# Band attention of the sample rows in plain float32, its four head pairs on four 32-column groups of the array

## The chip, the core and the metric

The kernel runs on one core of a Trainium2 chip. [...] The metric is the device time of one execution in microseconds (us). Three runs of the kernel before gave 1215.79, 1216.45 and 1216.54; the median is 1216.45.

## What is computed

One step of a streaming encoder layer: 512 prompt rows and 8 sample sequences of 16 new rows each, all float32. After one shared input projection there are two attention branches (A: latent attention; B: attention over a band of keys), then a gated merge, an output projection and a SwiGLU feed-forward part. The change lies in branch B of the sample rows. Each of the 8 sequences has 512 cached keys and values and 16 new ones, 8 heads of 64:

```python
def softmax_attend(q, k, v, bias):
    scale = q.shape[-1] ** -0.5
    s = jnp.einsum('bqhd,bkhd->bhqk', q, k).astype(jnp.float32) * scale + bias
    p = jax.nn.softmax(s, axis=-1).astype(v.dtype)
    return jnp.einsum('bhqk,bkhd->bqhd', p, v)

def band_sample(q, k_new, v_new, k_buf, v_buf, rel_bias, past_len):
    ...
    k = jnp.concatenate([k_buf, k_new], axis=1)
    v = jnp.concatenate([v_buf, v_new], axis=1)
    kpos = jnp.concatenate([past_len - W + jnp.arange(W), past_len + jnp.arange(Sd)])
    qpos = past_len + jnp.arange(Sd)
    return softmax_attend(q, k, v, band_bias(rel_bias, qpos, kpos)[None])
```

## The kernel before

Most products are not plain float32. An operand is split into a high part, rounded to the type float32r, and a low part, the rest (`split`, lines 83 to 89: a copy on ScalarE for the high part, a subtraction on VectorE for the low one), and a product is three matmuls: high by high, high by low, low by high (`mm3`, lines 91 to 94). Transposes go through TensorE (line 138) into PSUM tiles `tr` (4 of them); products go into PSUM tiles `mm` (4 of them). `granule` (line 178) loads 512 KB into one of three buffers `w_raw` and splits it.

The sample stage (from line 799) goes through the 8 sequences in one loop (line 1018). Each turn does the scores of one sequence for both branches and the values of the sequence before; the order of the operations is written out in a string (line 1019), and a scheduler may move instructions within what the dependencies allow. In the string, capital letters are work on this sequence, small ones on the one before:

- `N` (`band_start`, line 928): GpSimd copies the 16 queries of the sequence into the zeroed tiles `Qbd`, high and low. Per head pair the stationary is 128 x 128, of which 32 columns (2 heads x 16 queries) hold values; it takes two PSUM tiles for the scores.
- `K0` to `K3` (`band_keys`, line 937): per head pair, four transposes of cached keys, the split into `kTh` and `kTl`, and the 16 new keys by GpSimd (lines 947, 948).
- `S0` to `S3` (`band_scores`, line 951): per pair and half of the 528 keys three matmuls of 264 columns; the four pairs add up in one PSUM tile of 128 rows.
- `X` (`band_softmax`): bias, maximum, exponential, scaling by the sum (lines 961 to 964, 842 to 850, 646 to 650).
- `P` (`band_probs`, line 966): five transposes of the probabilities, split into pieces of 32 high and 32 low columns.
- `v0` to `v3` (`band_values`, line 977): per pair, five key blocks, the 64-column stationary against the high and the low part of the cached values (lines 987, 988); `o` (`band_out`, line 993): four transposes and the addition of the two parts.
- `K` without a digit, `Y`, `p`, `u`: keys, scores, transposed probabilities and values of the latent branch. `mla_values` (line 919) is in plain float32: its probabilities and cached latents are not split (line 924). In the first turn `absorb` (line 825) has plain float32 products too (line 834), on 64 rows of the array at a time: rows 0 to 63 for one set of four matmuls, rows 64 to 127 for the next.

The queries and new keys reach the stage transposed, with the other work of the projections, as `qbT`, `qbTl`, `kbT`, `kbTl` (`pair_T`, line 491).

```python
for op in "N K0 S0 v0 K1 v1 S1 K2 S2 v2 K3 S3 X p v3 K u o Y P A".split():
```

Of the kernel before, what the change touches and what calls it, by code (L numbers as in the profile page):

```python
# [9 lines left out]
F32R = mybir.dt.float32r  # L10
# [37 lines left out]
def layer_kernel(  # L48
# [47 lines left out]
    def rsqrt(out, ss, inv, pl, n):  # L96
        v = pl.tile([P, n], F32, tag="rs_v", bufs=2, name=nm("rsv"))
        t = pl.tile([P, n], F32, tag="rs_t", bufs=2, name=nm("rst"))
        if not isinstance(inv, list):
            inv = [(0, n, inv)]  # L100
        for a, b, sc in inv:
            V.tensor_scalar(out=v[:, a:b], in0=ss[:, a:b], scalar1=sc, scalar2=EPS, op0=ALU.mult, op1=ALU.add)
        # a square root of the scalar engine's table, then a Newton step to float32
        for a, b, sc in inv:
            S.activation(out=t[:, a:b], in_=ss[:, a:b], func=AF.Sqrt, scale=sc, bias=eps_t)
        V.reciprocal(out, t)
        V.tensor_tensor(out=t, in0=out, in1=out, op=ALU.mult)  # L107
        V.scalar_tensor_tensor(out=t, in0=t, scalar=-0.5, in1=v, op0=ALU.mult, op1=ALU.mult)
        V.scalar_tensor_tensor(out=out, in0=t, scalar=1.5, in1=out, op0=ALU.add, op1=ALU.mult)
# [10 lines left out]
    # ---------------------------------------------------------------- constants  # L120
# [10 lines left out]
    # the tensor engine's clock rises while the first loads are under way  # L131
# [29 lines left out]
    # weight staging: 0.5 MB granules, each split exactly into a high and a low part  # L161
# [58 lines left out]
    # ---------------------------------------------------------------- state of the sample up to its attention  # L220
# [6 lines left out]
    qbT, qbTl = sbt([P, 4, P], "qbT", F32R), sbt([P, 4, P], "qbTl", F32R)  # L227
    kbT, kbTl = sbt([P, 4, P], "kbT", F32R), sbt([P, 4, P], "kbTl", F32R)
# [25 lines left out]
    # ---------------------------------------------------------------- modulation, normed input, norms of cached keys  # L254
    with pool("klat") as kp, pool("xin") as xp:
# [79 lines left out]
        # h^T = xn^T * A + B, split  # L335
# [27 lines left out]
    # small constants of the attention part  # L363
# [38 lines left out]
    def split3(dst, src, order):  # L402
        # parts of src, 32 columns each, side by side: high and low parts in the order given
        first = order.index("h")
        hi = dst[:, :, first * 32:(first + 1) * 32]
        S.copy(hi, src)
        for i, o in enumerate(order):
            d = dst[:, :, i * 32:(i + 1) * 32]
            if o == "h" and i != first:
                S.copy(d, src)  # L410
            elif o == "l":
                V.tensor_tensor(out=d, in0=src, in1=f(hi), op=ALU.subtract)

    # ---------------------------------------------------------------- projections out of the modulated input
# [8 lines left out]
    with pool("cwork") as cw:  # L423
# [67 lines left out]
        def pair_T(hi, lo, src, scale):  # L491
            pt = tr_tile()
            for j in range(4):
                transpose(pt[:, j * P:(j + 1) * P], src[:, j * P:(j + 1) * P])
            split(hi, lo, pt.rearrange("p (j n) -> p j n", j=4), scale)

        def epi_qb(t, ps):
            qn = head_norm(ps)
            if t < 4:
                nc.sync.dma_start(qb_d[t * P:(t + 1) * P, :], qn)  # L500
            else:
                pair_T(qbT, qbTl, qn, gqb128)

        def epi_kb(t, ps):
# [7 lines left out]
            else:  # L512
                nc.sync.dma_start(bk_s[0].rearrange("s q h d -> (s q) (h d)"), kb)
                pair_T(kbT, kbTl, kb, None)
# [116 lines left out]
    # relative-bias table, its clipped far end extended, distance rising along the row  # L631
# [20 lines left out]
    # ---------------------------------------------------------------- attention of the prompt, beside the gates  # L652
# [5 lines left out]
    def gate_block(blk, pl):  # L658
        # sigmoid(z) = (1 + tanh(z / 2)) / 2; the sum and the factor come with the merge
# [25 lines left out]
    with pool("pwork") as pw:  # L685
# [17 lines left out]
        def head_in(n):  # L703
            br, h = n // H, n % H
            st = {"br": br, "h": h, "bias": None}
            if h % 2 == 0:
                vn = load_nat(vb_d if br else va_d, P, h // 2 * P, "vnat")
                # stationary of a head: its high and low parts side by side, the high part at the head's rows
# [90 lines left out]
    # ---------------------------------------------------------------- attention of the sample  # L799
    e2 = {}  # L800
    with pool("ework") as ew:
# [17 lines left out]
        Qbd = [et([P, 640], f"qbd{p}", 1, F32R) for p in range(2)]  # L819
        for q_ in Qbd:  # L820
            G.memset(f(q_), 0.0)
        vbh, vbl = et([P, 512], "vbh", 1, F32R), et([P, 512], "vbl", 1, F32R)
        split(vbh, vbl, vb_n)

        def absorb():
            # q' = Wk (g qn) per head
# [101 lines left out]
        def band_start(s):  # L928
            new = slice(s * DSEQ, (s + 1) * DSEQ)
            for p, src in ((0, qbT), (1, qbTl)):  # L930
                for h2 in range(2):
                    r = slice(64 * h2, 64 * h2 + 64)
                    G.tensor_copy(Qbd[p][r, :].rearrange("p (j x) -> p j x", x=160)[:, :, h2 * DSEQ:(h2 + 1) * DSEQ],
                                  f(src[r, :, new]))
            return {"s": s, "ps": [mm_tile(), mm_tile()]}

        def band_keys(st, pr_):
# [7 lines left out]
            hi, lo = et([P, KEYS], "kTh", 3, F32R), et([P, KEYS], "kTl", 3, F32R)  # L945
            split(hi[:, :PAST], lo[:, :PAST], pt)
            G.tensor_copy(hi[:, PAST:], f(kbT[:, pr_, new]))
            G.tensor_copy(lo[:, PAST:], f(kbTl[:, pr_, new]))
            st["k", pr_] = hi, lo

        def band_scores(st, pr_):
            hi, lo = st["k", pr_]
            ps_ = slice(pr_ * P, (pr_ + 1) * P)
            for hf in range(2):
                ks = slice(hf * KH, (hf + 1) * KH)
                mm3(st["ps"][hf][:, :KH], Qbd[0][:, ps_], Qbd[1][:, ps_], hi[:, ks], lo[:, ks], pr_ == 0, pr_ == 3)
# [9 lines left out]
        def band_probs(st):  # L966
            # per pair of heads: stationary [high | low] parts of its 32 rows of probabilities
            PT = et([P, 20, 2, 32], "PTb", 1, F32R)

            def evac(js, src):  # L970
                r, v = slice(4 * js.start, 4 * js.stop), src.rearrange("p j (a x) -> p (j a) x", x=32)
                split(PT[:, r, 0, :], PT[:, r, 1, :], v)

            probs_T(*st["P"], evac)
            st["PT"] = PT

        def band_values(st, pr_):
            if pr_ == 0:
                st["po"] = mm_tile()
            c = slice(pr_ * P, (pr_ + 1) * P)  # L980
            if pr_ % 2 == 0:
                st["v"] = granule(wa, cache_band_v[0, st["s"]].rearrange("(j p) h d -> p j (h d)", p=P)
                                  [:, :, pr_ * P:(pr_ + 2) * P], [4, 2 * P])
            vh, vl = [a[:, :, (pr_ % 2) * P:(pr_ % 2 + 1) * P] for a in st["v"]]
            for j in range(5):
                lhs = st["PT"][:, 4 * j + pr_].rearrange("p a x -> p (a x)")
                T.matmul(st["po"][:64, c], lhs, vh[:, j, :] if j < 4 else vbh[:, c], start=(j == 0), stop=False)
                T.matmul(st["po"][:64, c], lhs, vl[:, j, :] if j < 4 else vbl[:, c], start=False, stop=(j == 4))
            if pr_ == 3:
                st["o2"] = et([64, 512], "o2", 1)  # L990
                S.copy(st["o2"], st["po"][:64, :])

        def band_out(st):
            s = st["s"]
            pt = tr_tile()
            for pr_ in range(4):
                transpose(pt[:, pr_ * 64:(pr_ + 1) * 64], st["o2"][:, pr_ * P:(pr_ + 1) * P])
            pv = pt[:, :256].rearrange("p (j a x) -> p j a x", a=2, x=32)
            ol = et([P, 4, 32], "ol", 1)
            S.copy(ol, pv[:, :, 1, :])  # L1000
            c = slice(SEQ + s * DSEQ, SEQ + (s + 1) * DSEQ)
            for h2 in range(2):
                r, q = slice(64 * h2, 64 * h2 + 64), slice(h2 * DSEQ, (h2 + 1) * DSEQ)
                V.tensor_tensor(out=oT[1][r, :, c], in0=pv[r, :, 0, q], in1=ol[r, :, q], op=ALU.add)
# [8 lines left out]
        # operations of a step: lower case on the sequence before, upper case on this one  # L1013
# [4 lines left out]
        for s in range(NSEQ + 1):  # L1018
            for op in "N K0 S0 v0 K1 v1 S1 K2 S2 v2 K3 S3 X p v3 K u o Y P A".split():
                k, a = op[0], [int(c) for c in op[1:]]  # L1020
                if k.islower():
# [3 lines left out]
                    elif k == "v":  # L1025
                        take(1)
                elif s < NSEQ:
# [4 lines left out]
                    elif k == "S":  # L1032
                        band_scores(nxt, *a)
# [29 lines left out]
    # ---------------------------------------------------------------- merge of the branches  # L1063
# [18 lines left out]
    def gate_rows(c0, scale):  # L1082
        # rows of a gate, by tokens: of the prompt, of the sample
# [59 lines left out]
    # ---------------------------------------------------------------- output projection, residual, second norm  # L1143
# [79 lines left out]
    # ---------------------------------------------------------------- feed-forward  # L1223
# [61 lines left out]
def _tables():  # L1285
    """Rotary tables of the positions, and selectors of the modulation rows: of the shapes alone."""
# [40 lines left out]
```

## Time and profile before

| | |
|---|---|
| median of three runs | 1216.45 us |
| profiled execution, its span | 1215.7 us |
| TensorE busy | 1189.0 us, 98% |
| VectorE, ScalarE, GpSimd busy | 684.2, 544.3, 137.9 us |
| moved by DMA | 155.30 MB, 128 GB/s on average |
| turns of the sample stage after the first | 116.1 us, 15.25 us for one in the middle |

The profile is one execution. [...] The idle time shown in brackets is that just before an instruction, with what ended it.

### The profile page before, as it was taken

The numbers are of one execution on the slowest core, as the hardware profiler recorded it, in microseconds if no ns is written. First come the engines' busy times: TensorE is split into PE (matmuls) and PEld (weight loads), VectorE is DVE, ScalarE is ACT, GpSimd is POOL, SyncE is SP. The second block draws the span as 40 slices with busy tenths as digits, with TensorE's granted clock in tenths as the row PEclk, the third lists the DMA queues.
The fourth block names the chain that finished last, engine by engine and source line by source line (L and its number), as shares of the span: only waits on it lengthen the run. The fifth ranks groups of instructions, "written<-read, shape, count | busy, mean of one in ns | idle before, by whom it ended". The sixth has DMA issues, their size and how long they took to land. (4 is left out here: it accounts for less than half of the span.)

```text
span 1215.7 us, 19702 instructions
## 1 busy us (share of the span) xinstructions
PE 1189.0 (98%) x7515; PEld 1077.5 (89%) x7515; DVE 684.2 (56%) x1539; ACT 544.3 (45%) x1086; POOL 137.9 (11%) x253
## 2 busy tenths in 40 slices
PE   8889999999999999999999998999999999999998
PEld 6568988999987889899989888999989999889996
DVE  4887566858887775777766437433344233342333
ACT  6775533446776665666653246322112222112210
POOL 2440001010000101334212221000000000000000
PEclk9998999999999999999999998999999999999999
DMA  8651434475655348455367312322123222232111
GB/s 260 227 161 46 127 137 136 159 235 167 184 162 176 119 137 287 138 178 173 95 213 266 103 55 70 88 70 78 62 70 105 70 71 87 67 89 70 70 40 65
DMA packets 159264, 155.30 MB, mean 128 GB/s; under 512 B 24632, under 2 KB 123475, under 8 KB 159170
## 3 DMA queue, kind: packets, MB, share of 16 engines
q1 hardware_dynamic: 159170, 154.05, 40.4%
q8 instruction: 59, 0.97, 0.3%
q14 instruction: 35, 0.29, 0.1%
HBM read 135.15 MB, written 18.88 MB: 127 GB/s over the span
## 5 line engine op out<-in xcount | busy, mean ns | idle before, releaser
L85 ACT CAST whi<-wraw 128x1024 fp32r<-128x1024 f32 (+2 forms) x184 | 190.3, 1038 | 273.4 <-PE mm L94 107.5
L86 DVE TENSOR_TENSOR wlo<-wraw,whi 128x1024 fp32r<-128x1024 f32 (+3 forms) x168 | 203.4, 1213 | 131.6 <-ACT whi L85 127.3
L92 PE MATMUL mm<-h2T,whi 128*128 128x320 f32 x704 | 217.9, 311 | 0.0
L93 PE MATMUL mm<-h2Tl,whi 128*128 128x320 f32 x704 | 217.8, 310 | 0.0
L94 PE MATMUL mm<-h2T,wlo 128*128 128x320 f32 x704 | 217.8, 310 | 0.0
L92 PEld LDWEIGHTS mm<-h2T,whi 128*128 128x128 f32 x704 | 132.9, 189 | 0.4 <-ACT aT L85 0.4
L93 PEld LDWEIGHTS mm<-h2Tl,whi 128*128 128x128 f32 x704 | 132.7, 189 | 0.1
L94 PEld LDWEIGHTS mm<-h2T,wlo 128*128 128x128 f32 x704 | 132.7, 189 | 0.0
L1237 DVE TENSOR_TENSOR sg<-mm,sg 128x320 f32<-128x320 f32 x44 | 21.6, 492 | 121.3 <-PE mm L94 119.3
L93 PE MATMUL mm<-wlo,aT 128*128 128x512 f32 x220 | 85.5, 389 | 0.0
L92 PE MATMUL mm<-whi,aT 128*128 128x512 f32 x220 | 85.5, 389 | 0.0
L94 PE MATMUL mm<-whi,aTl 128*128 128x512 f32 x220 | 85.4, 389 | 0.0
L92 PE MATMUL mm<-hT_hi,whi 128*128 128x320 f32 x256 | 81.5, 318 | 0.0
L94 PE MATMUL mm<-whi,hT_lo 128*128 128x512 f32 (+3 forms) x240 | 79.6, 332 | 0.0
L94 PE MATMUL mm<-hT_hi,wlo 128*128 128x320 f32 x256 | 79.5, 311 | 0.0
L93 PE MATMUL mm<-hT_lo,whi 128*128 128x320 f32 x256 | 79.4, 310 | 0.0
L92 PE MATMUL mm<-whi,hT_hi 128*128 128x512 f32 (+3 forms) x240 | 79.4, 331 | 0.0
L93 PE MATMUL mm<-wlo,hT_hi 128*128 128x512 f32 (+3 forms) x240 | 79.4, 331 | 0.0
L1268 DVE TENSOR_TENSOR tmp<-mm,gate 128x512 f32<-128x512 f32 x30 | 20.7, 690 | 78.7 <-PE mm L94 78.7
L85 ACT CAST aT<-sg 128x320 fp32r<-128x320 f32 x44 | 20.0, 455 | 78.7 <-DVE sg L1237 78.7
L92 PEld LDWEIGHTS mm<-hT_hi,whi 128*128 128x128 f32 x256 | 48.2, 188 | 2.1 <-issue 1.2
L94 PEld LDWEIGHTS mm<-hT_hi,wlo 128*128 128x128 f32 x256 | 48.1, 188 | 1.2 <-DVE wlo L86 0.3
(343 smaller groups left out, 2672.4 us busy)
## 6 DMA issues: line engine op xcount, KB each, us to landing
wraw<-in_w_ada_dram SPq DMA_DIRECT2D x48, 512.0 KB
wraw<-in_w_in_dram SPq DMA_DIRECT2D x28, 512.0 KB
wraw<-in_w_gate_dram SPq DMA_DIRECT2D x22, 512.0 KB
wraw<-in_w_up_dram SPq DMA_DIRECT2D x22, 512.0 KB
wraw<-in_w_down_dram SPq DMA_DIRECT2D x22, 512.0 KB
lat<-in_cache_kv_latent_dram SPq DMA_DIRECT2D x16, 512.0 KB
wraw<-in_cache_band_v_dram SPq DMA_DIRECT2D x16, 512.0 KB
kn<-in_cache_band_k_dram SPq DMA_DIRECT2D x16, 512.0 KB
```

The source lines that it names most:

```text
L85: S.copy(hi, src)
L86: (eng or V).tensor_tensor(out=lo, in0=src, in1=f(hi), op=ALU.subtract)
L92: T.matmul(out, lh, rh, start=start, stop=False)
L93: T.matmul(out, lh, rl, start=False, stop=False)
L94: T.matmul(out, ll, rh, start=False, stop=stop)
L1237: V.tensor_tensor(out=sg, in0=pu[:, :HALF], in1=sg, op=ALU.mult)
L1268: V.tensor_tensor(out=tmp, in0=ps, in1=gate2[t // 4][:, cc], op=ALU.mult)
```

## The change

The band branch of the sample rows no longer splits anything. Queries and new keys are kept in plain float32 (`qbd`, `kbT`); `qbd` holds for each sequence and head pair a stationary of 128 rows and 32 columns, two blocks of 64 rows x 16 queries. The scores of a pair go to 32 rows of the PSUM tile of their own, which is a 32-column group of the array: pair 0 to rows 0 to 31, pair 3 to rows 96 to 127, one plain float32 matmul per pair and half, none adding to another. All eight come after the four pairs' keys. The transposed keys are one copy, by VectorE for even pairs and by ScalarE for odd ones, in six buffers. The probabilities are one copy; the values are loaded by halves of the keys instead of by halves of the heads, used as loaded, and each pair's product of 32 x 128 goes to its own 32 rows of one PSUM tile. The output is one transpose and two copies. The order of a step has two operations `v` instead of four and one `S` after the keys.

```diff
-    qbT, qbTl = sbt([P, 4, P], "qbT", F32R), sbt([P, 4, P], "qbTl", F32R)
-    kbT, kbTl = sbt([P, 4, P], "kbT", F32R), sbt([P, 4, P], "kbTl", F32R)
+    qbd, kbT = sbt([P, 4, NSEQ, 32], "qbd"), sbt([P, 4, P], "kbT")
+    G.memset(qbd, 0.0)
...
-                pair_T(qbT, qbTl, qn, gqb128)
+                pv = pair_T(qn).rearrange("p j (s q) -> p j s q", q=DSEQ)
+                for h2 in range(2):
+                    r = slice(64 * h2, 64 * h2 + 64)
+                    S.activation(out=qbd[r, :, :, h2 * DSEQ:(h2 + 1) * DSEQ], in_=pv[r], func=AF.Copy, scale=gqb128[r])
...
-                pair_T(kbT, kbTl, kb, None)
+                S.copy(kbT, pair_T(kb))
...
-        Qbd = [et([P, 640], f"qbd{p}", 1, F32R) for p in range(2)]
-        for q_ in Qbd:
-            G.memset(f(q_), 0.0)
-        vbh, vbl = et([P, 512], "vbh", 1, F32R), et([P, 512], "vbl", 1, F32R)
-        split(vbh, vbl, vb_n)
...
         def band_start(s):
-            new = slice(s * DSEQ, (s + 1) * DSEQ)
-            for p, src in ((0, qbT), (1, qbTl)):
-                for h2 in range(2):
-                    r = slice(64 * h2, 64 * h2 + 64)
-                    G.tensor_copy(Qbd[p][r, :].rearrange("p (j x) -> p j x", x=160)[:, :, h2 * DSEQ:(h2 + 1) * DSEQ],
-                                  f(src[r, :, new]))
-            return {"s": s, "ps": [mm_tile(), mm_tile()]}
+            return {"s": s}
...
-            hi, lo = et([P, KEYS], "kTh", 3, F32R), et([P, KEYS], "kTl", 3, F32R)
-            split(hi[:, :PAST], lo[:, :PAST], pt)
-            G.tensor_copy(hi[:, PAST:], f(kbT[:, pr_, new]))
-            G.tensor_copy(lo[:, PAST:], f(kbTl[:, pr_, new]))
-            st["k", pr_] = hi, lo
-
-        def band_scores(st, pr_):
-            hi, lo = st["k", pr_]
-            ps_ = slice(pr_ * P, (pr_ + 1) * P)
+            kT = et([P, KEYS], "kT", 6)
+            (S.copy if pr_ % 2 else V.tensor_copy)(kT[:, :PAST], pt)
+            G.tensor_copy(kT[:, PAST:], kbT[:, pr_, new])
+            st["k", pr_] = kT
+
+        def band_scores(st):
+            st["ps"] = [mm_tile(), mm_tile()]
             for hf in range(2):
-                ks = slice(hf * KH, (hf + 1) * KH)
-                mm3(st["ps"][hf][:, :KH], Qbd[0][:, ps_], Qbd[1][:, ps_], hi[:, ks], lo[:, ks], pr_ == 0, pr_ == 3)
+                for pr_ in range(4):
+                    T.matmul(st["ps"][hf][32 * pr_:32 * pr_ + 32, :KH], qbd[:, pr_, st["s"], :],
+                             st["k", pr_][:, hf * KH:(hf + 1) * KH], start=True, stop=True)
...
         def band_probs(st):
-            PT = et([P, 20, 2, 32], "PTb", 1, F32R)
-            def evac(js, src):
-                r, v = slice(4 * js.start, 4 * js.stop), src.rearrange("p j (a x) -> p (j a) x", x=32)
-                split(PT[:, r, 0, :], PT[:, r, 1, :], v)
-            probs_T(*st["P"], evac)
+            PT = et([P, 5, P], "PTb", 2)
+            probs_T(*st["P"], lambda js, src: S.copy(PT[:, js, :], src))
             st["PT"] = PT
...
-        def band_values(st, pr_):
-            if pr_ == 0:
+        def band_values(st, half):
+            if half == 0:
                 st["po"] = mm_tile()
-            c = slice(pr_ * P, (pr_ + 1) * P)
-            if pr_ % 2 == 0:
-                st["v"] = granule(wa, cache_band_v[0, st["s"]].rearrange("(j p) h d -> p j (h d)", p=P)
-                                  [:, :, pr_ * P:(pr_ + 2) * P], [4, 2 * P])
-            vh, vl = [a[:, :, (pr_ % 2) * P:(pr_ % 2 + 1) * P] for a in st["v"]]
-            for j in range(5):
-                lhs = st["PT"][:, 4 * j + pr_].rearrange("p a x -> p (a x)")
-                T.matmul(st["po"][:64, c], lhs, vh[:, j, :] if j < 4 else vbh[:, c], start=(j == 0), stop=False)
-                T.matmul(st["po"][:64, c], lhs, vl[:, j, :] if j < 4 else vbl[:, c], start=False, stop=(j == 4))
-            if pr_ == 3:
-                st["o2"] = et([64, 512], "o2", 1)
-                S.copy(st["o2"], st["po"][:64, :])
+            vt = load_raw(cache_band_v[0, st["s"], half * 2 * P:(half + 1) * 2 * P].rearrange("(j p) h d -> p j (h d)", p=P),
+                          [2, 512])[1]
+            for j in range(2 + half):
+                jj = 2 * half + j
+                for pr_ in range(4):
+                    c = slice(pr_ * P, (pr_ + 1) * P)
+                    T.matmul(st["po"][32 * pr_:32 * pr_ + 32, :P], st["PT"][:, jj, 32 * pr_:32 * pr_ + 32],
+                             vt[:, j, c] if j < 2 else vb_n[:, c], start=(jj == 0), stop=(jj == 4))
+            if half:
+                st["o2"] = et([P, P], "o2", 2)
+                S.copy(st["o2"], st["po"][:, :P])
...
-            for op in "N K0 S0 v0 K1 v1 S1 K2 S2 v2 K3 S3 X p v3 K u o Y P A".split():
+            for op in "N K0 K1 v0 K2 K3 v1 S X p K u o Y P A".split():
...
                     elif k == "v":
-                        take(1)
+                        take(2)
```

In `band_out` one transpose of 128 x 128 and two copies by ScalarE stand in place of four transposes, a copy and two additions. `take` fills the first turn with blocks of the gates' projection; four times one became two times two.

## Rows read from the trace of the kernel before

**Rows 1.** The page: busy us (share) and instructions; GB/s in 40 slices:

```profile
PE 1189.0 (98%) x7515; PEld 1077.5 (89%) x7515; DVE 684.2 (56%) x1539; ACT 544.3 (45%) x1086; POOL 137.9 (11%) x253
...
GB/s 260 227 161 46 127 137 136 159 235 167 184 162 176 119 137 287 138 178 173 95 213 266 103 55 70 88 70 78 62 70 105 70 71 87 67 89 70 70 40 65
```

**Rows 2.** Stretches: length, busy PE, PEld, DVE, ACT, POOL, clock, DMA share, GB/s:

```profile
545.05:560.30 15.25, 14.90 (x145) 14.46 (x145) 11.38 (x32) 10.47 (x24) 6.11 (x22) 1.00 0.53 174
...
500.30:616.40 116.10, 112.29 (x1077) 106.59 (x1077) 83.95 (x216) 77.53 (x165) 38.35 (x141) 1.00 0.48 149
```

**Rows 3.** Groups of TensorE in one step: busy us, mean ns, idle before:

```profile
L924 PE MATMUL mm<-PT,lat 128*128 128x128 f32 x16 | 2.3, 275 | 0.0
...
L924 PE MATMUL mm<-PT,lat_n 128*128 128x128 f32 x4 | 0.8, 275 | 0.0
```

**Rows 4.** TensorE in order of time: start us, length us, count, idle before:

```profile
547.24 0.22 PE L988 MATMUL mm<-wlo,PTb 128*64 128x128 f32 x1
547.30 0.23 PE L987 MATMUL mm<-whi,PTb 128*64 128x128 f32 x1
547.36 0.34 PE L93 MATMUL mm<-kTl,qbd 128*128 128x264 f32 x1
...
554.96 1.06 PE L924 MATMUL mm<-PT,lat 128*128 128x128 f32 x8
...
556.29 0.46 PE L138 MATMUL tr<-ident,o 64*128 64x64 f32 x4
556.68 0.39 PE L908 MATMUL mm<-krT,qrT 96*128 96x264 f32 x1
...
557.03 0.28 PE L93 MATMUL mm<-lTl,qp 128*128 128x264 f32 x1
...
558.12 0.28 PE L94 MATMUL mm<-lTh,qpl 128*128 128x264 f32 x1
...
558.91 1.04 PE L138 MATMUL tr<-ident,kn 128*128 128x128 f32 x8
560.30 0.51 PE L92 MATMUL mm<-kTh,qbd 128*128 128x264 f32 x2 [0.35 <-ACT kTh L85]
```

**Rows 5.** The same view around the plain float32 products of the first turn:

```profile
488.38 2.26 PE L834 MATMUL mm<-qnT,wkT 64*128 64x128 f32 x24
490.57 1.09 PE L138 MATMUL tr<-ident,lat 128*128 128x128 f32 x8
491.59 1.16 PE L834 MATMUL mm<-qnT,wkT 64*128 64x128 f32 x8
492.68 0.66 PE L138 MATMUL tr<-ident,rnb 128*128 128x128 f32 x4
```

**Rows 6.** Groups of VectorE, ScalarE and GpSimd in the same step:

```profile
L86 DVE TENSOR_TENSOR kTl<-tr,kTh 128x512 fp32r<-128x512 f32 x4 | 2.6, 682 | 1.2 <-ACT kTh L85 1.2
L86 DVE TENSOR_TENSOR wlo<-wraw,whi 128x1024 fp32r<-128x1024 f32 x2 | 2.4, 1222 | 0.0
...
L650 DVE TENSOR_SCALAR Pr<-Pr,sm 128x528 f32<-128x528 f32 x2 | 1.0, 498 | 0.6 <-DVE sm L649 0.5
...
L910 DVE CUSTOM_DVE_ANT_0 S<-mm,S 128x264 f32<-128x264 f32 x2 | 0.8, 426 | 0.0
...
L85 ACT CAST kTh<-tr 128x512 fp32r<-128x512 f32 x5 | 2.9, 602 | 2.1 <-POOL kTl L948 1.8 <-PE tr L138 0.4
L85 ACT CAST whi<-wraw 128x1024 fp32r<-128x1024 f32 x2 | 2.1, 1058 | 0.0
...
L947 POOL CAST kTh<-kbT 128x16 fp32r<-128x16 f32 x4 | 1.7, 463 | 0.0
```

**Rows 7.** VectorE and ScalarE in order of time, in the band's softmax:

```profile
555.86 0.14 DVE L844 TENSOR_REDUCE nmax<-mx 128x1 f32<-128x2 f32 x1
...
556.10 0.74 ACT L648 ACTIVATE Pr<-S,nmax 128x528 f32<-128x528 f32 x1 [0.64 <-DVE nmax L844]
```

More of the change, by code (lines that the diff above doesn't have):

```diff
@@ L489, in head_norm, with pair_T @@
             return qn
-        def pair_T(hi, lo, src, scale):
+        def pair_T(src):
             pt = tr_tile()
@@ L494, in pair_T @@
                 transpose(pt[:, j * P:(j + 1) * P], src[:, j * P:(j + 1) * P])
-            split(hi, lo, pt.rearrange("p (j n) -> p j n", j=4), scale)
+            return pt.rearrange("p (j n) -> p j n", j=4)
         def epi_qb(t, ps):
@@ L995, in band_out @@
             pt = tr_tile()
[L996 to L1000, printed above, removed]
+            transpose(pt[:, :P], st["o2"])
+            pv = pt[:, :P].rearrange("p (j x) -> p j x", x=32)
             c = slice(SEQ + s * DSEQ, SEQ + (s + 1) * DSEQ)
             for h2 in range(2):
-                r, q = slice(64 * h2, 64 * h2 + 64), slice(h2 * DSEQ, (h2 + 1) * DSEQ)
-                V.tensor_tensor(out=oT[1][r, :, c], in0=pv[r, :, 0, q], in1=ol[r, :, q], op=ALU.add)
+                r = slice(64 * h2, 64 * h2 + 64)
+                S.copy(oT[1][r, :, c], pv[r, :, h2 * DSEQ:(h2 + 1) * DSEQ])
         def step_0():
@@ L1032, in layer_kernel @@
                     elif k == "S":
-                        band_scores(nxt, *a)
+                        band_scores(nxt)
                     elif k == "X":
```

## The prediction

> **What bounds the kernel now.** I began with the busy times of the page: TensorE is busy 98% of the span [rows 1], so an instruction taken off it shortens the run unless something takes its place, and work taken off the other engines is worth little by itself. Then the stage that the change touches, stretch by stretch: eight sequences, a step of 15.25 us for each in the middle and 116.1 us for all but the first turn [rows 2]. [...] Next the groups of one step, for counts [rows 3], and the order of time, for what an instruction really takes from TensorE: not its duration (matmuls overlap) but the distance from one start to the next [rows 4].
>
> **What is removed, per sequence.** The old scores are 2 halves x 4 pairs x 3 products = 24 matmuls of 264 columns. Ten of the same shape stand in a row from 557.03 to 558.12, 0.121 us apart [rows 4]: 24 x 0.121 = 2.90 us. The old values are 4 pairs x 5 key blocks x 2 parts = 40 matmuls of 128 columns, 0.06 us apart [rows 4]: 2.40 us. The four transposes of the output take from 556.29 to 556.68, 0.39 us [rows 4]. Sum 5.69 us.
>
> **What is added, per sequence.** A plain float32 product in this stage is that of the latent values, L924. The code has 10 such matmuls per step, the trace 16 + 4 = 20 records [rows 3]: a float32 matmul is two records. Eight take 1.06 us, the last alone 0.28, so 0.112 us per record of 128 columns [rows 3, 4]. In proportion a record of 264 columns takes 0.23 us. The new scores are 8 matmuls = 16 records, the new values 20 matmuls = 40 records.
> What these cost hangs on how far the four column groups run at once. No row shows column groups. One end is none at once: 16 x 0.23 + 40 x 0.112 = 3.68 + 4.48 = 8.16 us. The other is all four: scores 2 x 2 x 0.23 = 0.92, values 5 x 2 x 0.112 = 1.12. The nearest row is L834, float32 matmuls on 64 of the 128 rows, where neighbouring sets of eight records lie on different halves of the rows. Eight alone take 1.16 us; three such sets in succession take 2.26 us for 24 records [rows 5], where 1.16 + 16 x 0.112 = 2.95 would be one after the other. The 0.69 us saved are six records, three at each of the two borders: the end of one set ran beside the start of the next. So two parts of the array do run two-record matmuls at once. I therefore go by the "all four" end. For the values I leave a surcharge, since 40 weight loads and matmuls must be issued in 1.12 us while the closest such pairs in a row start 0.06 us apart (40 x 0.06 = 2.40, the upper end): I take 1.3. Sum 2.22.
> [...]
> The output's transpose is now one instead of four: 0.11 (eight of 128 columns in 1.04 us [rows 4], the first seven 0.109 each).
> **Changing the array's division.** At L834 the array goes from whole rows to half rows and back. The eight transposes that start at 490.57 need 8 x 0.109 = 0.87 us of distance, but the next group starts after 1.02; the eight of L834 after it need 0.90 and take 1.09 [rows 5]. So 0.15 to 0.19 us per change. The old 64-column values show none: the scores after them start 0.06 us later [rows 4]. The new order has the first half of the values, then keys, then the second half of the values with the scores beside it: two stretches, four changes, 4 x 0.17 = 0.70 us (0.6 to 0.8).
> [...]
> **Other engines.** Off VectorE go four key splits and two value splits, 2.6 and 2.4 us [rows 6], and smaller ones; on come two key copies, at most 0.68 each: from 11.4 to under 8. Off ScalarE go four key casts of 0.60 and two of 1.06 [rows 6], on come two key copies of 0.60: from 10.5 to about 7. Both lie far under TensorE. These microseconds are worth at most the 0.35 us that TensorE waits for a key cast at a step's start [rows 4]; I count that at nothing, since the copy in its place takes as long.
> **New waits.** The scores now need all four key copies at once, where before each pair's scores needed its own. Queued behind them on TensorE stand the latent probabilities and keys, and for them wait VectorE (the band's softmax) and thereby the step. The last pair's copy (0.60, with GpSimd's 16 columns beside it, 0.46 [rows 6]) is covered by the second half of the values, 12 of 20 matmuls or 0.78 us, and one change, 0.17. With a hand-over of about 0.1 on either side (VectorE's maximum ends at 556.00, ScalarE's exponential starts at 556.10 [rows 7]) that is just enough. The latent softmax has the tighter cover, see the rivals. I take 0.3 us per step for new waits, between 0 and 1.0.
> **Loads.** A step still loads 2 x 512 KB of keys, 2 x 512 KB of values and one latent block, issued in the same order on SP's queue; the value granules are cut by keys instead of by columns. 174 GB/s become about 206 at a step of 12.9 us, at a share of 0.63 instead of 0.53 [rows 2]; a slice of the page reaches 287 [rows 1]. A value granule's buffer is now held until TensorE has read it, not just until its split: with three buffers and two granules per step the next load still goes out about a step ahead. I count nothing; without that cover, part of a load of 512 KB (about 2.5 us at 206 GB/s) would stand in a step. The GpSimd copies of the old query blocks and the one zeroing at the start lie beside other work.
>
> **The sum.** 0.92 + 1.30 + 0.11 + 0.70 + 0.30 - 5.69 = -2.36 us per sequence, x 8 = -18.9. The profiled execution goes from 1215.7 to 1196.8. The median of the runs, 1216.45, lies 0.75 above its span, so the time is 1197.5. With the good ends (1.12 for the values, 0.6 for the changes, no new wait, the 0.35 gone) a step loses 3.29: 1190. With 1.0 of new waits and 0.4 more issue in the values it loses 1.26: 1206.
>
> **The rivals.**
> *In order, two at a time.* If a waiting second record holds up the next group's first one, each matmul overlaps its neighbour by one record only: scores 9 x 0.23 = 2.07, values 22 x 0.112 = 2.46; with 0.11 and 0.70 that is 5.34, a gain of 0.35 x 8 = 2.8: 1213.6. For it: no row shows more than two parts at once. Against it: at L834 the overlap is three records at each border, not one [rows 5].
> [...]
> *One after the other: slower.* If column groups do not overlap in plain float32, each matmul fills 32 of 128 columns for its two records: 8.16 + 0.81 - 5.69 = +3.28 x 8 = +26: 1243. It decides where fewer than 8.16 / (5.69 - 0.81) = 1.67 groups run at once on average. For it: no row shows a column group, and the old form needs only 0.121 where one new float32 matmul alone needs 0.46. That the four groups are not used as groups at all comes to the same.
> *A softmax chain takes the place.* Between the latent scores and their transposed probabilities other engines need 2 x 0.43 after the last score, 0.14, 0.74 and 0.50 [rows 6, 7], three short instructions that I set at 0.15 like the maximum, some eight hand-overs of 0.1, and perhaps two key copies (1.4) ahead in VectorE's queue: 4.9. TensorE's work between is the band's probabilities 5 x 0.109 = 0.55, 16 key transposes 1.74, then 1.30, 0.92 and 0.70: 5.2, where before it was 0.55 + 1.74 + 2.40 + 2.90 = 7.6. If more stands ahead in a queue, or if the final order scatters the grouped matmuls among transposes (eight more changes, 1.4 us), about 1.2 us per step are lost: 1207.
>
> **How the numbers follow.** All four at once 0.54 (1190 to 1206), chain or scattering 0.14 (1200 to 1214), in order 0.16 (1211 to 1216), one after the other 0.16 (1230 to 1250). Predicted is the likeliest, 1197.5. The range goes from 1190 to 1217 and leaves out the slow case and some edges. About 0.2% (2.4 us) is what a measurement of this kernel can tell from no change. Faster by more: 0.54 + 0.13 + 0.10 = 0.77; same: 0.01 + 0.06 = 0.07; slower: 0.16.
>
> **What would show it.** Right: steps of about 12.9 us; the score records of one half starting in close fours, a half done in about 0.5 us; a value block every 0.22 to 0.26 us; four breaks of 0.17 us per step. In order: a start every 0.23 or 0.112 us, steps of 14.9. One after the other: the same distances over twice the time, steps of 18.5. Chain: TensorE idle ahead of the latent probabilities, released by VectorE's scaling. The prediction is wrong if the score starts of a half stand 0.23 us apart eight times over.

## The result and the profile after

The changed kernel takes 1196.8 us (median of 4, 1195.4 to 1202.0) beside 1216.1 us for the kernel before on the same chip: a ratio of 0.985, 95% interval 0.983 to 0.988. Forecast were 1197.5 us, range 1190 to 1217. The profiled execution, the fastest of the four, went from 1215.7 to 1193.7 us of span: 22.0 us less, where the medians differ by 19.3. The total was right, but its parts were not: the stage gave more than forecast, and another stage gave part of it back.

The busy times on the page of the changed kernel, the line that answers to [rows 1]:

```profile
PE 1163.5 (97%) x7427; PEld 1045.2 (88%) x7427; DVE 650.9 (55%) x1472; ACT 521.1 (44%) x1062; POOL 106.5 (9%) x188
```

Two middle steps by stretches, the columns as in [rows 2]:

```profile
536.24:547.60 11.36, 10.97 (x133) 10.18 (x133) 6.63 (x23) 7.49 (x20) 2.24 (x14) 1.00 0.71 231
547.60:558.97 11.37, 10.99 (x133) 10.21 (x133) 6.63 (x23) 7.48 (x20) 2.24 (x14) 1.00 0.69 230
```

A step takes 11.37 us, where 15.25 stood in [rows 2] and 12.9 was forecast. TensorE in order of time in such a step (start, length, count, idle before), the view of [rows 4]:

```profile
545.23 1.08 PE L972 MATMUL mm<-wraw,PTb 128*32 128x128 f32 x32
546.13 0.40 PE L972 MATMUL mm<-vb_n,PTb 128*32 128x128 f32 x8
546.35 1.09 PE L947 MATMUL mm<-kT,qbd 128*32 128x264 f32 x16
547.83 0.63 PE L138 MATMUL tr<-ident,Pr 128*128 128x128 f32 x4 [0.39 <-DVE Pr L654]
548.29 0.27 PE L138 MATMUL tr<-ident,Pn 128*128 128x128 f32 x1
```

All 40 value records and 16 score records stand in one stretch, from 545.23 to about 547.44. The 40 value records need 1.12 us, ten rounds of 0.11: four groups at once. Then TensorE waits 0.39 us for the latent softmax, as the "chain" rival named it, at about the price the forecast gave to new waits (0.3).

Summing the distances from each start on TensorE to the next, by kind, over one middle step:

| us per step | before | after | forecast of the difference | measured |
|---|---|---|---|---|
| band scores | 3.39 | 1.09 | 0.92 - 2.90 = -1.98 | -2.30 |
| band values | 2.57 | 1.12 | 1.30 - 2.40 = -1.10 | -1.45 |
| transposes of the output | 0.39 | 0.03 | 0.11 - 0.39 = -0.28 | -0.36 |
| all else, changes of the division with it | 8.52 | 8.74 | +0.70 | +0.22 |
| idle | 0.35 | 0.39 | +0.30 | +0.04 |
| sum | 15.22 | 11.37 | -2.36 | -3.85 |

Three points of the run cut it into parts: the first product of the absorbed queries (L834 before, L832 after), the first of the latent outputs (`mm<-olatT,wraw`), and the last `mm<-oh,whi` of the merge. Lengths in us, from single executions; the last four rows are kernels of the next section:

| | start to absorbed queries | to latent outputs | to the end of the merge | to the end |
|---|---|---|---|---|
| before | 488.4 | 128.0 | 67.3 | 532.0 |
| after | 488.6 | 101.9 | 73.1 | 530.2 |
| after, once more | 487.6 | 101.3 | 74.2 | 531.3 |
| zeroing on VectorE | 485.6 | 101.7 | 74.2 | 530.7 |
| rows loaded early | 486.3 | 103.3 | 67.2 | 530.9 |
| both | 487.4 | 103.2 | 67.4 | 532.1 |

The sample stage gave 26.1 us. The merge, in which nothing was changed, took 5.8 us more. Its rows, TensorE in order of time, and two stretches with the clock as the column before the DMA share:

```profile
590.42 3.84 PE L1037 MATMUL mm<-olatT,wraw 128*128 128x128 f32 x32 [0.46 <-ACT olatT L924]
598.99 2.34 PE L211 MATMUL tr<-sel,wraw 19*128 19x9 f32 x16 [2.29 <-DMA wraw<-in_b_ada_dram]
...
596.00:606.00 10.00, 7.71 (x39) 7.46 (x39) 6.18 (x12) 6.63 (x15) 0.00 (x0) 0.72 0.63 188
606.00:616.00 10.00, 10.00 (x66) 9.79 (x66) 5.93 (x10) 3.49 (x6) 2.76 (x3) 0.94 1.02 395
```

TensorE waits 2.29 us for a small load, and in the 20 us of the two stretches the granted clock is 0.50 for a part (from about 600.3 to 607.1 us): (0.28 + 0.06) x 10 = 3.4 us of clock lost. In a second execution of the changed kernel the wait was 3.63 us, and the clock of the same two stretches 0.66 and 0.99. SP's queue, on which these loads are issued, shows why the load is late:

```profile
591.97 1.77 SPq L1100 DMA_DIRECT2D g<-gate_d  x4
593.85 0.29 SPq L1060 DMA_DIRECT2D wraw<-ada_d  x1
594.18 0.25 SPq L1061 DMA_DIRECT2D wraw<-in_b_ada_dram  x1
```

Four loads of the gates stand ahead of it. In the kernel before the two small loads went out at 616.77, ahead of the gate loads at 620.04, and the products on them ran without a wait at 620.18, with no stretch at a lower clock behind them (the granted clock is 1.00 from 616 to 636 us):

```profile
616.77 0.30 SPq L1078 DMA_DIRECT2D wraw<-ada_d  x1
617.12 0.25 SPq L1079 DMA_DIRECT2D wraw<-in_b_ada_dram  x1
...
620.04 1.79 SPq L1118 DMA_DIRECT2D g<-gate_d  x4
...
620.18 1.95 PE L211 MATMUL tr<-sel,wraw 19*128 19x9 f32 x16
```

Why the order on the queue is another is not shown. The length of the stage alone does not set it: the kernel with the scores on one group, below, takes 117.7 us for the stage and has the gate loads first too.

### The profile page after: what moved, and what is told of

The parts are those of the page before. It is cut to its first block, busy times and chain, and to the rows that moved or that the text cites. A ratio compares the mean times of both kernels' runs of the same rounds, so it can differ in the third digit from the quotient of the medians.

```text
span 1193.7 us, 19291 instructions
## 1 busy us (share of the span) xinstructions
PE 1163.5 (97%) x7427; PEld 1045.2 (88%) x7427; DVE 650.9 (55%) x1472; ACT 521.1 (44%) x1062; POOL 106.5 (9%) x188
## 5 line engine op out<-in xcount | busy, mean ns | idle before, releaser
L85 ACT CAST whi<-wraw 128x1024 fp32r<-128x1024 f32 (+3 forms) x168 | 173.2, 1037 | 274.6 <-PE mm L94 108.0
L86 DVE TENSOR_TENSOR wlo<-wraw,whi 128x1024 fp32r<-128x1024 f32 (+3 forms) x152 | 182.5, 1203 | 134.4 <-ACT whi L85 131.3
L92 PEld LDWEIGHTS mm<-whi,hT_hi 128*128 128x128 f32 x240 | 45.2, 188 | 6.5 <-ACT jk L320 2.9
```

Of the source, the lines that this page charges most:

```text
L86: (eng or V).tensor_tensor(out=lo, in0=src, in1=f(hi), op=ALU.subtract)
L92: T.matmul(out, lh, rh, start=start, stop=False)
```

## Experiments

**Do the four groups make the saving? The scores on one group.**

```diff
-    T.matmul(st["ps"][hf][32 * pr_:32 * pr_ + 32, :KH], ...
+    T.matmul(st["ps"][hf][:32, :KH], ...          # both tiles zeroed by VectorE before
```

> The changed kernel, but the scores of all four pairs are written by one column group, one over the other (three quarters of the scores are thereby left out, and VectorE zeroes the two score tiles ahead). The number and the shape of the matmuls stay. Theory G (the saving comes from four column groups at once): 16 records of 0.22 to 0.23 us in a row, 3.6 us instead of 1.1: step +2.5, to about 13.9 us, the run about 20 us above the changed kernel. Rival N (the eight score matmuls are cheap for another reason, such as 32 stationary columns): no change, step 11.4 us. A zeroing that stands in the way of the scores would show as TensorE waiting for VectorE there.

Measured: 1215.5 us, 19 above the changed kernel; step 13.57. TensorE in order of time:

```profile
545.73 3.72 PE L949 MATMUL mm<-kT,qbd 128*32 128x264 f32 x16
549.39 0.66 PE L138 MATMUL tr<-ident,Pr 128*128 128x128 f32 x4
```

The same 16 records, now 0.222 us from start to start, take 3.65 us instead of 1.09. The distance is the same between the last record of the first half and the first of the second, which write to different PSUM tiles, so it is the group that they share and not the place they write to. The step grows by 2.2 and not by 2.56, because the longer scores cover the 0.39 us wait. Theory G holds. The groups, not the 32 columns, save the time; this is also the price of the "one after the other" rival.

**The scores twice: what do 16 more records cost?**

```diff
-            for hf in range(2):
+            for hf in (0, 1, 0, 1):
```

> The changed kernel with each sequence's eight score matmuls run twice, the second time over the first: the price of the disputed product by itself, without a further change of the division. Theory G (four groups at once): 16 more records at 0.22 / 4 each, 0.9 us per step, 7 us in all (the step 12.3 us). Rival I (in order, two at a time): 2.07 us per step, 17 us. Rival O (one after the other): 3.6 us per step, 29 us.

Measured: 1198.8 us (1194.7 to 1200.3), step 11.83:

```profile
535.23 1.98 PE L947 MATMUL mm<-kT,qbd 128*32 128x264 f32 x32
537.14 0.65 PE L138 MATMUL tr<-ident,Pr 128*128 128x128 f32 x4
```

32 records take 1.91 us: eight rounds of four, 0.222 us from round to round, and 0.13 at the end. On one group 0.222 is the time of each record, so four groups give the full factor of four, and theory G holds. The step grew by 0.46 only, since the repeated scores fill the 0.39 us wait; the expectation had left that out.

**How far out of order? The values pair by pair.**

```diff
-            for j in range(2 + half):
-                for pr_ in range(4):
+            for pr_ in range(4):          # when both halves are loaded
+                for jj in range(5):
```

> The changed kernel, but the 20 value matmuls of a sequence stand pair by pair: the five key blocks of one pair, ten records on one column group, before the next pair, all issued when the second half of the values is there. Theory W (the array takes records out of their order only as far ahead as a short waiting room, about three records as at the float32 sets on half rows): a group's records run one after another, only the last three of a pair beside the first of the next, about 31 slots of 0.11 us = 3.4 instead of 1.1 us: step +2.3, to 13.7 us, the run about 18 us above the changed kernel. Rival F (the array finds work for an idle group however far ahead): no change, step 11.4 us, within 2 us of the changed kernel.

Measured: 1207.1 us, 10.3 above the changed kernel; step 12.95. TensorE in order of time, the first pair and the second's start:

```profile
553.88 1.09 PE L973 MATMUL mm<-wraw,PTb 128*32 128x128 f32 x10
554.78 0.27 PE L973 MATMUL mm<-vb_n,PTb 128*32 128x128 f32 x1
554.81 0.27 PE L973 MATMUL mm<-wraw,PTb 128*32 128x128 f32 x1
554.89 0.27 PE L973 MATMUL mm<-vb_n,PTb 128*32 128x128 f32 x1
554.92 0.74 PE L973 MATMUL mm<-wraw,PTb 128*32 128x128 f32 x7
```

Each pair's ten records still follow one another by 0.109, and the next pair starts 0.685 us after the one before, when seven of ten have started (553.880, 554.565, 555.250, 555.935): pair 1's first record starts ahead of pair 0's last three. So about three records wait here at the occupied group before what stands behind them gets a turn, as at the half rows of [rows 5]. The values take 2.99 us instead of 1.12. Theory W holds. It cost 1.6 us per step and not 2.3, because the first scores start beside the last pair (556.62, before its last records at 556.94) and the 0.39 us wait is filled. The order in which the change issues its matmuls, group by group in turn, is worth 10 us of its 20.

**One part alone: only the new values.**

```diff
-"N K0 K1 v0 K2 K3 v1 S X p K u o Y P A"
+"N K0 S0 v0 K1 S1 K2 S2 v1 K3 S3 X p K u o Y P A"      # keys split, scores in three products as before
```

> Only the new values: probabilities and cached values in plain float32 on four column groups, one output transpose; keys split and scores in three products as before. Read by a middle step. Values go from 2.40 to about 1.1 us, the transposes from 0.39 to 0.11, changes of the division cost 0.24: 1.35 less. Theory A (the remaining gaps belong to the keys): step about 13.9 us, stage 11 us shorter. Rival B (gaps belong to the value splits): step about 13.2 us, stage 16 us shorter. The zeroing at the start is then the old one inside the stage, so the first 100 us should run as before, not 2 us later.

Measured: 1215.8 us; ratio to before 0.999, interval 0.998 to 1.001. A middle step takes 13.81. The sum is near that of theory A (13.9), its parts are not: the values take 1.70 us where about 1.1 was expected (they stand in three stretches among the old scores), the old scores 3.74 where they took 3.39 before, and the 0.35 us of idle time is gone. The stage ended some 8 us earlier than before, where theory A had 11; the merge gave that back.

**The other part alone: only the new scores.**

```diff
-"N K0 K1 v0 K2 K3 v1 S X p K u o Y P A"
+"N K0 v0 K1 v1 K2 v2 K3 v3 S X p K u o Y P A"      # values split and by 64 columns as before
```

> Only the new scores: keys not split, scores in plain float32 on four column groups; values, their splits and the four output transposes as before. Read by the length of a middle step (before 15.25, after the whole change 11.4 us). By the prices of the changed trace the scores go from 2.90 to about 1.1 us and two changes of the division cost 0.24: 1.57 less. Theory A (the further 0.7 us that a step lost are gaps between matmuls that waited for key casts and key splits): the step loses 2.3, to about 13.0 us, and the stage about 18 us. Rival B (those gaps belong to the value granules and their splits): the step loses 1.6, to about 13.7 us, the stage about 12.5 us. The start's zeroing on GpSimd stays, so about 2 us are lost there in both.

Measured: 1217.2 us; ratio 1.000, interval 0.999 to 1.002. A middle step takes 14.7: only 0.55 less, and both expectations miss. Three rows of TensorE show two causes:

```profile
558.41 0.27 PE L982 MATMUL mm<-whi,PTb 128*64 128x128 f32 x1 [0.59 <-DVE PTb L86]
559.93 1.08 PE L950 MATMUL mm<-kT,qbd 128*32 128x264 f32 x8
563.02 1.08 PE L950 MATMUL mm<-kT,qbd 128*32 128x264 f32 x8
```

The scheduler put pairs 0 and 1 in one stretch and pairs 2 and 3 in another. Each runs on two groups and takes as long as all four together, so the scores cost 2.03 us. And TensorE waits 0.59 us for the low parts of the probabilities. The two parts alone bring 0.55 and 1.4 us per step; together they bring 3.85.

**The new scores alone, in one stretch.**

```diff
-"N K0 v0 K1 v1 K2 v2 K3 v3 S X p K u o Y P A"
+"N K0 K1 K2 K3 v0 v1 v2 v3 S X p K u o Y P A"
```

> Again only the new scores (values, splits and output transposes as before), but all four keys ahead of the values, so that a sequence's eight score matmuls stand in one stretch; in the run with only the new scores the order had pairs 0 and 1 in one stretch and pairs 2 and 3 in another, each two groups at a time, 1.01 us each. Theory P (that pairing is why the scores alone brought 0.55 us per step instead of 1.6): the scores take about 1.1 us once, 0.9 to 1.1 us less per step, a middle step of 13.6 to 13.8 us. Rival Q (the 0.59 us wait for the low parts of the probabilities and other waits bound that step): 14.4 to 14.7 us as there.

Measured: 1220.1 us, ratio 1.003 (1.002 to 1.005): slower than before. Step 14.74. TensorE, then VectorE, ScalarE and GpSimd, in order of time:

```profile
544.35 1.10 PE L950 MATMUL mm<-kT,qbd 128*32 128x264 f32 x16
546.73 0.52 PE L138 MATMUL tr<-ident,Pr 128*128 128x128 f32 x3 [1.29 <-DVE Pr L654]
547.83 0.33 PE L138 MATMUL tr<-ident,Pn 128*128 128x128 f32 x1 [0.47 <-POOL Pn L850]
...
544.18 1.23 DVE L86 TENSOR_TENSOR wlo<-wraw,whi 128x1024 fp32r<-128x1024 f32 x1 [1.03 <-ACT whi L85]
545.33 0.16 DVE L653 RECIPROCAL sm<-sm 128x1 f32<-128x1 f32 x1
545.40 0.41 DVE L957 CUSTOM_DVE_ANT_0 S<-mm,biasd 128x264 f32<-128x264 f32 x1
545.74 0.43 DVE L957 CUSTOM_DVE_ANT_0 S<-mm,biasd 128x264 f32<-128x264 f32 x1
546.09 0.49 DVE L654 TENSOR_SCALAR Pr<-Pr,sm 128x528 f32<-128x528 f32 x1
546.50 1.22 DVE L86 TENSOR_TENSOR wlo<-wraw,whi 128x1024 fp32r<-128x1024 f32 x1
...
543.10 1.05 ACT L85 CAST whi<-wraw 128x1024 fp32r<-128x1024 f32 x1
544.05 0.74 ACT L652 ACTIVATE Pr<-S,nmax 128x528 f32<-128x528 f32 x1
...
546.65 1.13 POOL L850 COPY Pn<-Pr 128x16 f32<-128x16 f32 x1 [5.26 <-DVE Pr L654]
```

Theory P's scores are there, 1.10 us, but the gain is gone: TensorE idles 1.76 us in a step: 1.29 ahead of the latent probabilities' transposes and 0.47 for a small copy by GpSimd. The exponential of the latent softmax stands on ScalarE behind the cast of a value granule (1.05 us), its reciprocal on VectorE behind the split of one (1.23), and its scaling behind the band's two bias additions as well (545.40 to 546.09). In the changed kernel the scaling (547.19) stands ahead of those additions (547.60). GpSimd's copy takes 1.13 us beside the next split, and 0.20 in the changed kernel. Rival Q is nearer than theory P, though the step is still a little longer than Q's 14.4 to 14.7 and the wait is another: with fewer matmuls to cover it, the softmax chain sets the step. By these rows casts and splits have a large part in the 1.4 us of idle time that this kernel has more than the changed one (1.76 - 0.39), though both engines are far from full. How large is not shown, since no run takes them away without changing the values and the order too.

**Scattered: the latent keys ahead of the latent probabilities.** This kernel and the next have the two repairs below besides.

```diff
-"N K0 K1 v0 K2 K3 v1 S X p K u o Y P A"
+"N K0 K1 v0 K2 K3 v1 S X K p u o Y P A"
```

> The version with the zeroing on VectorE and the early rows, and the latent keys ordered ahead of the latent probabilities to fill the 0.38 us in which TensorE waits for the softmax. The order of TensorE that comes of it has the eight score matmuls in three pieces with whole-array transposes between them, and the values in three pieces. Theory D (each further change of the division costs 0.1 to 0.2 us, and a piece that ends on two groups leaves the others idle): four to six changes and about 0.5 us of idle groups against 0.38 saved: the step grows from 11.37 to 12.0 to 12.6 us. Rival E (changes are free, the wait was all): the step falls to about 11.0 us.

Measured: 1212.2 us, 21 above the same kernel without the new order (1190.8, below); step 15.0: 3.6 more, where theory D gave 0.6 to 1.2. TensorE in order of time, the scores of one sequence:

```profile
557.15 0.84 PE L949 MATMUL mm<-kT,qbd 128*32 128x264 f32 x6
557.92 0.66 PE L138 MATMUL tr<-ident,lat 128*128 128x128 f32 x4
558.51 1.08 PE L949 MATMUL mm<-kT,qbd 128*32 128x264 f32 x4
559.52 0.65 PE L138 MATMUL tr<-ident,lat 128*128 128x128 f32 x4
560.01 0.49 PE L138 MATMUL tr<-ident,rnb 128*128 128x128 f32 x3
560.43 1.08 PE L949 MATMUL mm<-kT,qbd 128*32 128x264 f32 x4
```

By distances the scores take 2.88 us instead of 1.09: pairs 0 and 1 stand in one piece, pairs 2 and 3 in one each, and a piece of one pair (four records in a row at 0.222) takes 1.01, as long as all eight matmuls together. The values take 0.40 more, the changes among the rest and at the output 1.18, idle time 0.26. Theory D has the sign, but the idle groups cost 1.79 at the scores alone where the expectation had 0.5.

**The scores ahead of the values.**

```diff
-"N K0 K1 v0 K2 K3 v1 S X p K u o Y P A"
+"N K0 K1 K2 K3 S v0 v1 X p K u o Y P A"
```

> The version with the zeroing on VectorE and the early rows, and the scores ordered ahead of the values: in the order that comes of it the score and value matmuls stand mixed in one stretch, the last score matmuls ahead of the last eight value matmuls. Theory W (the 0.38 us wait per step is the softmax chain after the scores, and work of about 0.4 us behind them covers it): a middle step of about 11.0 us, 7 steps by 0.37, 2.6 us less: about 1188. Rival X (mixed on one group, a score record of 0.22 us holds up value records of 0.11 on the same group and the others idle, since only about four records are taken out of order): the step stays at 11.4 us or grows, 1190 to 1194.

Measured: 1199.0 us, 8 above the 1190.8; step 12.39. Rival X has the sign, but at most 1194 was expected. Scores and values mixed take 1.32 + 1.73 = 3.05 us instead of 2.21, and TensorE then waits 0.32 us for ScalarE's copy of the latent probabilities. That long records on a group hold short ones back, as rival X has it, fits, though with the values pair by pair about three records waited where it has four; no run shows it by itself.

**The loss at the merge: the rows of the shift loaded early.**

```diff
+    b2rows = ot.tile([19, DM], F32, tag="b2rows", name="b2rows")
...
+        nc.sync.dma_start(b2rows[0:18, :], ada_d[:, 3 * DM:4 * DM])      # before wv32
+        nc.sync.dma_start(b2rows[18:19, :], b_ada[:, 3 * DM:4 * DM])
...
-                ada_shift(B2, ada_cols(ada_rows(3 * DM), 8))
+                ada_shift(B2, ada_cols(b2rows, 8))
```

> The changed kernel, but the rows of the second norm's shift are loaded early into a buffer of their own, so that their load no longer stands behind four gate loads on SP's queue. Theory L (at 599 us TensorE waits 2.3 us for this load, then runs 6.8 us at half clock, about 3.4 us): the wait goes and the clock stays at its upper level there: 5 to 6 us less, about 1191. Rival C (the clock falls there in any case, because the stage before is less dense): only the wait goes, 2 to 2.5 us less, about 1194.5. Rival M (another load of the same queue is late next): no gain.

Measured: 1193.3 us (1189.4 to 1195.4), ratio to before 0.980 (0.978 to 0.983). TensorE in order of time, then two stretches:

```profile
584.50 1.95 PE L211 MATMUL tr<-sel,b2rows 19*128 19x9 f32 x16
...
591.00:601.00 10.00, 7.86 (x55) 7.08 (x54) 7.84 (x18) 9.49 (x24) 0.00 (x0) 1.00 0.71 236
601.00:611.00 10.00, 10.00 (x69) 9.79 (x68) 5.87 (x11) 2.33 (x4) 3.40 (x3) 1.00 0.92 341
```

The wait and the low clock are both gone; the part from the latent outputs to the end of the merge is 67.2 us, against 73.1 and 74.2 for the changed kernel and 67.3 before (table above). The 16 small products now stand in the part before, which is 1.4 to 2.0 longer. That is what theory L expected: the wait is gone and the granted clock stays at 1.00 in the two stretches. The gain is smaller than the 5 to 6 us expected: net 4 to 5 us in the traces, 3.0 to 3.5 by the medians (1193.3 beside 1196.8 and 1196.3).

**The loss at the start: zeroing on VectorE.**

```diff
-    G.memset(qbd, 0.0)
+    V.memset(qbd, 0.0)
```

> The changed kernel, but the block-diagonal query tile is zeroed by VectorE, which has nothing to do until 8.8 us, instead of by GpSimd between the two instructions that make the identity. Theory S (the 0.95 us zeroing holds the identity up, with it the first matmuls, and the order of the first 100 us follows): warm-up matmuls start at about 1.35 instead of 2.21 us, the products after 100 us run about 2 us earlier, the run ends about 2 us earlier (1195). Rival R (the 2 us come from another order of the first loads and products, or from the clock alone): warm-up earlier, the products after 100 us not.

Measured: 1194.2 us, ratio 0.982 (0.980 to 0.984); the changed kernel beside the next runs had 0.983 (0.981 to 0.985), so the totals can't be told apart. GpSimd and TensorE in the changed kernel, then TensorE here:

```profile
0.87 0.95 POOL L229 MEMSET qbd<- 128x1024 f32 x1
1.86 0.29 POOL masks.py:199 TENSOR_SCALAR_AFFINE_SELECT ident<-ident 128x128 f32<-128x128 f32 x1
2.21 4.93 PE L134 MATMUL tr<-ident 128*128 128x128 f32 x24 [2.21 <-POOL ident masks.py:199]
...
1.36 4.80 PE L134 MATMUL tr<-ident 128*128 128x128 f32 x24 [1.36 <-POOL ident masks.py:199]
```

TensorE starts 0.85 us earlier. Whether that reaches the stage stays open: the absorbed queries come at 488.6, 487.6 and 486.3 us with the zeroing on GpSimd, at 485.6 and 487.4 with it on VectorE, and at 487.5 and 489.6 in the two versions above that have it there too. The low stretches of the granted clock in the first 110 us lie otherwise in the profiles of the two kernels: in stretches of 10 us that begin at 10, 30, 50 and 60 us it is 0.83, 0.83, 0.88 and 0.78 in the changed one, in those that begin at 30 and 90 us 0.83 and 0.66 in the one before.

**Both repairs, and the changed kernel once more.**

> Both: zeroing by VectorE, and the rows of the shift loaded early. If the two losses are independent, the gains add: about 7 to 8 us under the changed kernel, 1189, which is what the prediction's 18.9 us less in the stage plus the 9.6 us more that the stage gave would make it. If one replaces the other (the clock's low stretch only moves), 1192 to 1195.

> The changed kernel itself once more, beside the others: 1196.8 us as before, the yardstick for the two versions of this set.

Measured: 1190.8 us (1188.6 to 1192.9), ratio 0.979 (0.977 to 0.981), and 1196.3 us, ratio 0.983 (0.981 to 0.985) for the changed kernel. The version with both beats both kernels. It is about 5.5 us below the changed one. The 1190.8 lie between the two cases of the expectation (1189, and 1192 to 1195) and does not decide between them. The stage gave 7.2 us more than the forecast (26.1 - 18.9), not the 9.6 that the expectation has.

## Why the prediction came out right, and where it did not

**What bounds, and the four groups: right.** TensorE set the step, and four column groups ran at once in plain float32, read off from half rows of the array [rows 5]. The scores on one group and the scores twice show it: 0.222 us per record on one group, 0.222 per round of four on four. "In order, two at a time" and "one after the other" are out, though no more than two groups ran at once where the matmuls stood badly: pair by pair (0.685 us from pair to pair), or two pairs in a stretch (2.03 us for the scores).

**The size of the step's gain: too small by 1.49 us.** By the table: 0.32 at the scores, 0.35 at the values, 0.08 at the transposes, 0.48 at the changes, 0.26 at idle time. The old scores and values were costed at the distances inside clean rows (0.121, 0.06) [rows 4]; over a whole step they took 3.39 and 2.57, since they stood in pieces among other shapes. The surcharge of 0.18 for issuing 40 values did not exist (1.12, not 1.30), nor did four changes at 0.17: values and scores stood in one stretch, which is two changes, and all the rest of the step grew by 0.22.

**"Other engines count nothing": wrong in its reason.** The prediction let the splits off VectorE and ScalarE be worth at most 0.35 us. In the kernel with the new scores in one stretch they stay, and TensorE idles 1.76 us per step. Its rows put cast and split into the chain of the latent softmax, but how much of the idle time is theirs alone stays open. The cover that the chain rival computed (5.2 against 4.9 us) fell 0.39 us short even with the value splits gone from those queues. The 0.35 us wait for a key cast, which the forecast kept, is gone; the 0.39 us for the softmax came in its place. The 0.3 that the forecast took for new waits was a choice between 0 and 1.0, so that it came near 0.39 proves little.

**Chain or scattering: the mechanism right, its price too low.** The chain's wait is real, 0.39 us. Scattering was set at 1.2 us per step; the one scattered order that was run cost 3.6, since a piece on one group takes 1.01 us where the whole on four takes 1.09.

**Loads count nothing, and no term for the clock: wrong by about 6 us.** The loads were argued for the stage alone, and the forecast has no term for the clock, which is 1.00 in the stretches of [rows 2]. In the merge, behind the stage, four gate loads now stand ahead of a small load on SP's queue, a wait of 2.3 us appeared, and behind it 6.8 us at a granted clock of 0.50. Loading the rows early takes both away.

**The sum.** Forecast 8 x 2.36 = 18.9 us of span, measured 22.0 (19.3 by the medians). The stage gave 26.1 between the two points of the table (less than 8 x 3.85 = 30.8: the first and the last turn gain less, in the last one TensorE waits 1.66 us for a key copy), the merge took 5.8, the rest gave 1.7. So the total came out near by luck: two errors of opposite sign, a stage that gave 7.2 us more and a merge that took 5.8.

## What to carry to other kernels

Here the small products on separate column groups paid their full factor where the matmuls of all groups stood together and took turns group by group (1.09 us for the scores, 1.12 for the values); on two groups at a time the scores took 2.03, and pair by pair the values took 2.99, so most of it was lost. Cost what is removed by its share of a whole step, not by its distance in the cleanest row, and ask of each engine that is relieved which chain stood in its queue. When a stage gets shorter, read the stage behind it: which loads now stand ahead of which on the queue, and whether the granted clock falls there (0.72 and 0.94 here).

## What the runs showed of the hardware

With the values pair by pair, the first record of a pair started 0.685 us after that of the pair before, where ten records take 1.09: about three records waited at the occupied group while records behind them, for another group, started. In the changed kernel the first four value records, on four groups, start at 545.234, 545.240, 545.247 and 545.254 us, 6 to 7 ns apart. Between the whole array and the four groups the distances were longer: in the changed kernel the first value record starts 0.203 us after a transpose where two transposes stand 0.109 apart, 0.09 more; with the scores twice the first transpose starts 0.317 us after the last score record where rounds stand 0.222 apart, 0.10 more, and 1.91 us after the first score record where eight rounds make 1.78, 0.13 more. GpSimd's copy of 16 columns, 0.20 us in the changed kernel, took 1.13 us beside a split on VectorE. After the wait in the merge the granted clock fell: with waits of 2.29 and 3.63 us in two executions of the changed kernel, it was 0.72 and 0.66 from 596 to 606 us. With the rows loaded early (1.00 from 591 to 611 us), and in the kernel before (1.00 from 616 to 636 us), there was neither the wait nor the fall. A wait alone did not always go with a fall: in the changed kernel TensorE waits 2.49 us before a product at 103.08 us, and the granted clock is 1.00 from 100 to 130 us. What makes it fall is not shown.
